# A mixing block on one core: the first phase's side transfers are issued by GpSimd instead of SP

## The chip, the core and the metric

The kernel runs on one core of a Trainium2 chip. A core has a matrix engine (TensorE, PE in the rows), a vector engine (VectorE, DVE), a scalar engine (ScalarE, ACT), GpSimd (POOL) and SyncE (SP), each with its own queue of instructions that it takes in order, and 16 DMA engines that move data between the chip's memory and the core. A transfer is issued by an instruction in the queue of one of the engines; here SP and GpSimd issue them all. The metric is the device time of one execution, in microseconds.

## The reference

One layer of a hybrid block: 2048 latent tokens and 256 context tokens of 1024 features. All arithmetic is fp32.

```
h_lat = rmsnorm(x_lat, norm1) * (1 + sc1) + sh1          # h_ctx likewise
q, k, v, gg, lr, lx, lg, su = split(h @ w_in)            # one input projection
gla  = gla_mixer(q, k, v, lr)       # gated linear attention, both directions
lru  = rglru_mixer(lx)              # short convolution, gated linear recurrence, both directions
s5   = s5_mixer(su)                 # 16 groups of 16 channels, 64 complex states each, both directions
mix  = concat(gated gla, gated lru, gated s5) @ w_out
x    = x + g1 * mix
h2   = rmsnorm(x, norm2) * (1 + sc2) + sh2
x    = x + g2 * (square(relu(h2 @ w1)) @ w2)             # MLP, 4096 wide
out  = rmsnorm(x, final_norm)
```

Each scan over the latent tokens starts from the final state of the context's scan, so it needs results of the input projection from far apart, and the backward directions need the last tokens first.

## The kernel before

**Products.** Every fp32 product of the projections is done as three products of split operands (`mm3`, L323 to L326): a weight tile is loaded by SP (`wsplit`, L318), ScalarE rounds it to its upper part (L319), VectorE takes the lower part (L320), and TensorE adds three matmuls into one accumulator. There are 2 raw buffers of weights, 2 of upper and 3 of lower parts.

**First phase** (up to about 850 us). The main stream is the input projection (`in_proj`) in four segments of 512 latent tokens and the context, followed by the output projection of the last segment (`out_proj(3)`). A finished accumulator (2 of them, `acc`) is copied by ScalarE into one of EV = 3 evacuation tiles (`evac`, L331) and stored to DRAM scratch: the parts su, lx, k, q, gg and lg by GpSimd (`put`, L343 to L355), the values v and the decay ranks by SP (`v_cols`, L385 and L394). Beside it run side streams, which read that scratch back:

- `xstream`: preparation of S5's matrices and phase tables (`s5_prep`, `s5_tables`; stores at L730 to L734 and L761), then 16 groups, one after the other (`s5_run`; loads at L770 to L774, matmuls at L783 and L820 to L824, the store of the result y at L829). A group takes 3 of 6 work slots, so two are in flight.
- `ystream`, `ystream2`: the first part of GLA by pairs of blocks (`gla_prep`, L873 to L953), with GpSimd's small copies at L906 to L913.
- the RG-LRU (`lru`, load L465, store L508), modulation vectors (`mod_rest`, weights loaded at L277), and the read-out of the last segment (`read_out(3)`, L1064 to L1142).

**Second phase**: the MLP of segments 3, 2, 1 and 0, with the RG-LRU's backward direction, read-out and output projection of the next segment beside it.

**Order.** `Streams` emits a step of a side stream whenever it is behind the main stream by planned step times. The tile framework then orders each engine's instructions by priority and by its own estimate of when operands are there, so that moving transfers to another queue also moves instructions on other engines. Each engine's queue goes strictly in order: an instruction that waits (a transfer whose source isn't written, or whose target buffer is in use) holds all that stand behind it. Transfers of one queue share 8 semaphores in turn, so each also waits for the eighth before it.

The lines that the prediction speaks of, as they stand before:

```
G.dma_start(dst[s][rows, :], e)                                       # L355 gg, lg, k, q
S.dma_start(v_d[s][sl, c * 256:(c + 1) * 256], ev[:, 0:256])          # L385 values
S.dma_start(tb, tb_d[g])                                              # L774 S5 tables of a group
S.dma_start(y_d[g // 8][:, gg * 16:(gg + 1) * 16, :, :], yo)          # L829
G.tensor_copy(c0s[:, :, two], hb_(s2)[:, :, :, 0])                    # L906
```

Of the kernel before, what the change touches and what calls it, by code (L numbers as in the profile page):

```python
# [8 lines left out]
F32 = mybir.dt.float32  # L9
# [33 lines left out]
# columns of the packed per-feature vector table  # L43
# [9 lines left out]
# W_in column tiles of 128 features  # L53
COLS = ["su0", "su1", "lx0", "lx1", "k0", "k1", "q0", "q1", "gg0", "gg1", "gg2", "gg3", "lg0", "lg1"]
WIDX = {n: i for i, n in enumerate(COLS)}
VN = 272         # half of v and the decay ranks of one direction


class Streams:
    """Emits a main and several side streams of instructions in step.  # L60

    A stream yields the time that its step takes, or the name of an event that has to be emitted first."""
# [10 lines left out]
    def step(self, limit):  # L73
        """One step of the side stream that is furthest behind; False if none is ready before `limit`."""
# [16 lines left out]
    def run(self, main):  # L91
        """`main` with the side streams."""
# [26 lines left out]
def hybrid_block(ctx: ExitStack, tc: tile.TileContext, xT, ctxT, cc, cct, wmodA, wmodT, pv, win, wva, wvb, upw, lrini, lruw, s5v, gluw,  # L119
# [27 lines left out]
    # ---------------------------------------------------------------- constants  # L147
# [53 lines left out]
    # ---------------------------------------------------------------- pools of the first phase  # L201
# [4 lines left out]
    def slots(tag, size, bufs):  # L206
        """A rotating workspace of `bufs` slots of `size` floats a partition."""
# [25 lines left out]
    # ---------------------------------------------------------------- adaLN vectors  # L233
# [3 lines left out]
    # silu(c) on every partition, for the products that run along the free axis  # L237
# [8 lines left out]
    def mod_first():  # L246
        """shift and scale of the first norm, latent and context"""
# [80 lines left out]
    # ---------------------------------------------------------------- input projection  # L328
# [40 lines left out]
    def v_cols(c, chunks):  # L369
        """Half of the values, token by token, with the decay ranks of one direction."""  # L370
        with tc.high_priority(WP):
            ws = [wsplit(ip, wv[c][:, j * 4 * VN:(j + 1) * 4 * VN], [4, VN], "w", WA) for j in range(2)]
        for s in chunks:
# [3 lines left out]
            for b in range(nb):  # L377
# [5 lines left out]
                with tc.high_priority(WP):  # L383
                    ev = evac(acc, VN)
                    S.dma_start(v_d[s][sl, c * 256:(c + 1) * 256], ev[:, 0:256])  # L385
# [1058 lines left out]
```

## Time and profile before

| | |
|---|---|
| Median of 3 runs | 2480.51 us (2476.40 to 2482.62) |
| Span of the profiled execution | 2482.1 us |
| TensorE busy | 2347.2 us (95%) |
| VectorE busy | 1610.0 us (65%) |
| ScalarE busy | 1169.2 us (47%) |
| GpSimd busy | 100.7 us (4%), 141 instructions |
| Transfers by SP's queue (hardware_dynamic) | 346.20 MB, 44.1% of the 16 engines' span |
| Transfers by GpSimd's queue (software_dynamic) | 15.93 MB, 1.9% |

The page gives the busy time of each engine and cuts the span into slices; the slices show a first third in which TensorE is not full and its clock is granted at less than full speed in pieces, and then a long stretch in which it is full. An issue of a transfer is written as DMA_DIRECT2D; on SP and in waits of SP the queue is called SPq. "L355 ... gg<-ev" reads: line 355, written tile or tensor gg, read tile ev.

### The profile page before, as it was taken

How to read it: one execution, taken by the hardware profiler on the slowest of the kernel's cores; microseconds unless marked ns; L12 is line 12 of the kernel's file. 1: busy time of each engine (PE TensorE's matmuls, PEld its weight loads, DVE VectorE, ACT ScalarE, POOL GpSimd, SP SyncE). 2: the span in 40 equal slices, each digit the busy share in tenths (PEclk: the TensorE clock that was granted, in tenths of full speed). 3: DMA queues.
4: the chain of work that ended last, by engine and by line, in shares of the span. 5: the costliest groups of instructions: out<-in, count | busy, mean ns of one | idle time of the engine just before them, and what ended most of it. 6: DMA issues, size and time to landing. Idle time of an engine off the chain costs nothing.

```text
span 2482.1 us, 29891 instructions
## 1 busy us (share of the span) xinstructions
PE 2347.2 (95%) x10992; PEld 1886.0 (76%) x10992; DVE 1610.0 (65%) x2698; ACT 1169.2 (47%) x1704; POOL 100.7 (4%) x141
## 2 busy tenths in 40 slices
PE   7779999898887899999999999999999999999997
PEld 3668777877675677888877788887778888888886
DVE  6886878726786766565576656557655655655555
ACT  3764567436555645343355534336543433433333
POOL 1020111002100000000000000000000000000000
PEclk9989999999998999999999999999999999999999
DMA  7666777557775643322355322336522232333221
GB/s 258 209 201 208 223 238 227 168 174 207 253 240 181 206 135 120 101 94 93 100 177 162 118 86 93 102 102 202 159 85 94 94 102 87 126 102 102 94 94 51
DMA packets 189107, 364.03 MB, mean 147 GB/s; under 512 B 35200, under 2 KB 104144, under 8 KB 187920
## 3 DMA queue, kind: packets, MB, share of 16 engines
q1 hardware_dynamic: 183872, 346.20, 44.1%
q0 software_dynamic: 5088, 15.93, 1.9%
q8 instruction: 86, 1.41, 0.2%
q14 instruction: 61, 0.50, 0.1%
HBM read 299.76 MB, written 62.75 MB: 146 GB/s over the span
## 4 chain that ended last, share of the span: by engine, by line
PE 64%; ACT 5%; DVE 5%; DMA 3%; issue 2%; SPq 1%; POOL 0%; DVEq 0%; ACTq 0%; POOLq 0%
PE acc L324 10%; PE acc L326 9%; PE acc L325 9%; PE sa L324 9%; PE sa L325 9%; PE sa L326 9%; PE sb L324 2%; PE sb L326 2%; PE sb L325 2%; DVE wL L320 1%; ACT wH L319 1%; PE sb L1146 1%; DMA t<-lru 1%; DMA t<-kk_d 0%; DMA wR<-in_wout_dram 0%
## 5 line engine op out<-in xcount | busy, mean ns | idle before, releaser
L319 ACT CAST wH<-wR 128x1024 fp32r<-128x1024 f32 (+1 forms) x353 | 370.9, 1051 | 903.9 <-PE sa L325 432.8
L324 PE MATMUL acc<-hH,wH 128*128 128x512 f32 (+1 forms) x1576 | 629.6, 400 | 24.8 <-ACT hH L303 9.2
L320 DVE TENSOR_TENSOR wL<-wR,wH 128x1024 fp32r<-128x1024 f32 (+1 forms) x353 | 427.3, 1222 | 346.5 <-ACT wH L319 342.0
L326 PE MATMUL acc<-hH,wL 128*128 128x512 f32 (+1 forms) x1576 | 620.1, 394 | 3.2 <-DVE wL L320 3.1
L325 PE MATMUL acc<-hL,wH 128*128 128x512 f32 (+1 forms) x1576 | 617.7, 392 | 1.2 <-DVE hL L307 0.8
L1257 DVE SCALAR_TENSOR_TENSOR xa<-sa,modl,xa 128x512 f32<-128x512 f32 (+1 forms) x520 | 383.1, 741 | 197.5 <-PE sa L326 194.8
L324 PE MATMUL sa<-sH,wH 128*128 128x512 f32 (+1 forms) x1040 | 403.9, 389 | 4.6 <-DVE xa L1257 4.2
L326 PE MATMUL sa<-sH,wL 128*128 128x512 f32 (+1 forms) x1040 | 402.2, 387 | 0.0
L325 PE MATMUL sa<-sL,wH 128*128 128x512 f32 (+1 forms) x1040 | 401.9, 386 | 0.0
L324 PEld LDWEIGHTS acc<-hH,wH 128*128 128x128 f32 x1576 | 299.8, 191 | 95.3 <-ACT hH L303 10.3
L325 PEld LDWEIGHTS acc<-hL,wH 128*128 128x128 f32 x1576 | 300.1, 191 | 70.8 <-issue 6.2
L326 PEld LDWEIGHTS acc<-hH,wL 128*128 128x128 f32 x1576 | 299.5, 190 | 70.8 <-DVE wL L320 5.2
L324 PEld LDWEIGHTS sa<-sH,wH 128*128 128x128 f32 x1040 | 195.2, 188 | 49.2 <-DVE xa L1257 9.3
L326 PEld LDWEIGHTS sa<-sH,wL 128*128 128x128 f32 x1040 | 195.3, 188 | 40.8
L325 PEld LDWEIGHTS sa<-sL,wH 128*128 128x128 f32 x1040 | 195.4, 188 | 40.6 <-DVE sL L1233 0.8
L1233 DVE TENSOR_TENSOR sL<-sr,sH 128x512 fp32r<-128x512 f32 x128 | 88.2, 690 | 27.6 <-ACT sH L1232 27.5
L325 PE MATMUL acc<-wL,hH 128*128 128x272 f32 x288 | 87.8, 305 | 8.8 <-DVE wL L320 8.7
L324 PE MATMUL acc<-wH,hH 128*128 128x272 f32 x288 | 89.2, 310 | 2.0 <-ACT ev L331 1.9
L331 ACT COPY ev<-acc 128x512 f32<-128x512 f32 (+2 forms) x96 | 47.5, 495 | 85.1 <-issue 41.0
L326 PE MATMUL acc<-wH,hL 128*128 128x272 f32 x288 | 86.5, 301 | 0.0
L1232 ACT CAST sH<-sr 128x512 fp32r<-128x512 f32 x128 | 78.8, 617 | 10.8 <-PE sa L326 9.0
L1231 ACT ACTIVATE sr<-sr 128x512 f32<-128x512 f32 x128 | 80.8, 632 | 3.4
(402 smaller groups left out, 2717.2 us busy)
## 6 DMA issues: line engine op xcount, KB each, us to landing
wR<-in_w_dram SPq DMA_DIRECT2D x256, 512.0 KB
wR<-in_win_dram SPq DMA_DIRECT2D x54, 512.0 KB
wm<-in_wmodT_dram SPq DMA_DIRECT2D x32, 512.0 KB
wR<-in_wout_dram SPq DMA_DIRECT2D x32, 512.0 KB
wm<-in_wmodA_dram SPq DMA_DIRECT2D x8, 1024.0 KB
x<-in_xT_dram SPq DMA_DIRECT2D x8, 1024.0 KB
w<-pk_d SPq DMA_DIRECT2D x16, 512.0 KB
xa<-in_xT_dram SPq DMA_DIRECT2D x32, 256.0 KB
```

The lines of the kernel that those rows point to most:

```text
L319: A.copy(Hf, raw)
L320: V.tensor_tensor(Lf, raw, f32(Hf), OP.subtract)
L324: T.matmul(acc, wH, hH, start=first, stop=False)
L325: T.matmul(acc, wH, hL, start=False, stop=False)
L326: T.matmul(acc, wL, hH, start=False, stop=last)
L331: A.copy(e, acc)
L1146: T.matmul(ps, gw[:, k, ct * P:(ct + 1) * P], sg[k], start=k == 0, stop=k == 1)
L1231: A.activation(r, r, AF.Square)
L1232: A.copy(sH, r)
L1233: V.tensor_tensor(sL, r, f32(sH), OP.subtract)
L1257: V.scalar_tensor_tensor(xa[:, m, a0:a1], acc, modl[:, 40 + m:41 + m], xa[:, m, a0:a1], OP.mult, OP.add)
```

## The change

In the first phase the transfers of the S5, GLA and RG-LRU streams, the stores of values and decay ranks, and the loads of the last segment's read-out are issued by GpSimd (`G`) instead of SP (`S`). SP keeps weights, tokens and constants, and in the second phase everything that it had. For `lru`, `back_step` and `read_out` the queue is now an argument, since both phases call them. All other edits remove comments.

```diff
-                    S.dma_start(v_d[s][sl, c * 256:(c + 1) * 256], ev[:, 0:256])
+                    G.dma_start(v_d[s][sl, c * 256:(c + 1) * 256], ev[:, 0:256])
...
-    def lru(d, order, wl=wl):
+    def lru(d, order, wl=wl, dq=G):
...
-                S.dma_start(xw[ct], src[ct * P:(ct + 1) * P, t0:t0 + n + 3])
+                dq.dma_start(xw[ct], src[ct * P:(ct + 1) * P, t0:t0 + n + 3])
...
-            S.dma_start(pk_d[gs, :, j * W:(j + 1) * W].rearrange("g p m -> p g m"),
+            G.dma_start(pk_d[gs, :, j * W:(j + 1) * W].rearrange("g p m -> p g m"),
...
-        S.dma_start(ur[:, 0:32], su_c[:, ch, :])
-        S.dma_start(ur[:, 32:288], su_l[:, ch].rearrange("s h r w -> s h (r w)"))
-        S.dma_start(pk, pk_d[g][:, 0:1024])
-        S.dma_start(tz, pk_d[g][:, 1024:])
-        S.dma_start(tb, tb_d[g])
+        G.dma_start(ur[:, 0:32], su_c[:, ch, :])
+        G.dma_start(ur[:, 32:288], su_l[:, ch].rearrange("s h r w -> s h (r w)"))
+        G.dma_start(pk, pk_d[g][:, 0:1024])
+        G.dma_start(tz, pk_d[g][:, 1024:])
+        G.dma_start(tb, tb_d[g])
...
-        S.dma_start(y_d[g // 8][:, gg * 16:(gg + 1) * 16, :, :], yo)
+        G.dma_start(y_d[g // 8][:, gg * 16:(gg + 1) * 16, :, :], yo)
...
-                S.dma_start(qq_d[(blk - 2) // 2], qd)
-                S.dma_start(kk_d[(blk - 2) // 2], kd)
+                G.dma_start(qq_d[(blk - 2) // 2], qd)
+                G.dma_start(kk_d[(blk - 2) // 2], kd)
...
+        dq = G if s == 3 else S
...
-            st.add(chain(lru(1, [s - 1], wide), read_out(s - 1), out_proj(s - 1)), RO)
+            st.add(chain(lru(1, [s - 1], wide, S), read_out(s - 1), out_proj(s - 1)), RO)
```

**SP's queue at the third S5 group, before.** The names: y is the S5 result, w_5283 and w_5282 the third group's work slots, qq_d and kk_d GLA's decayed queries and keys, wR a raw weight tile, pk_d and tb_d S5's matrices and tables.

```order
L829 DMA y_0_111<-w_5130 8x16x256
L770 DMA w_5283<-su_c_76 128x1x32
L917 DMA qq_d_115<-wg_5158 128x1024
L771 DMA w_5283<-su_l_75 128x1x256
L918 DMA kk_d_116<-wg_5155 128x1024
L318 DMA wR_6139<-in_win_dram 128x1024
L772 DMA w_5282<-pk_d_113 128x1024
L917 DMA qq_d_115<-sq_5182 128x1024
L918 DMA kk_d_116<-x_5180 128x1024
L318 DMA wR_6231<-in_win_dram 128x1024
L773 DMA w_5283<-pk_d_113 128x384
L774 DMA w_5283<-tb_d_114 128x320
```

**GpSimd's queue at the same loads, now**; c0s, x2s and a1s are the targets of GLA's small copies, gg an evacuation store of the input projection.

```order
L772 DMA w_5282<-pk_d_113 128x1024
L355 DMA gg_3_98<-ev_5679 128x512
L912 COPY a1s_158<-wg_5157 64x4x2
L913 COPY a1s_158<-wg_5157 64x4x2
L906 COPY c0s_156<-ssum_5181 128x4x2
L907 COPY x2s_157<-ssum_5181 64x4x2
L909 COPY x2s_157<-x_5180 64x4x2
L773 DMA w_5283<-pk_d_113 128x384
L774 DMA w_5283<-tb_d_114 128x320
```

The two weight loads and the four GLA stores no longer stand between the third group's loads; a store of the input projection and GLA's copies do.

**GpSimd's queue at the stores of lg of segment 1, before.** These rows are the input projection's evacuation stores, with two GLA copies.

```order
L355 DMA gg_1_96<-ev_3555 128x512
L355 DMA lg_1_100<-ev_3629 128x512
L355 DMA lg_1_100<-ev_3663 128x512
L346 DMA su_l_75<-ev_3777 128x8x64
L906 COPY c0s_156<-wg_3013 128x4x2
L907 COPY x2s_157<-wg_3013 64x4x2
L346 DMA su_l_75<-ev_3821 128x8x64
```

**The same queue from the same store on, now**; sf_d are GLA's forward states.

```order
L355 DMA gg_1_96<-ev_3555 128x512
L953 DMA sf_d_118<-fs_2980 64x512
L906 COPY c0s_156<-wg_3013 128x4x2
L907 COPY x2s_157<-wg_3013 64x4x2
L355 DMA lg_1_100<-ev_3629 128x512
L732 DMA pk_d_113<-w_3372 128x2x512
L909 COPY x2s_157<-wg_3012 64x4x2
L730 DMA pk_d_113<-w_3509 16x2x384
L912 COPY a1s_158<-wg_3013 64x4x2
L913 COPY a1s_158<-wg_3013 64x4x2
L730 DMA pk_d_113<-w_3509 16x2x384
L917 DMA qq_d_115<-wg_3014 128x1024
```

The copy L906 of the GLA block wg_3013 has moved ahead of three stores of the input projection, and the first of them now stands behind it.

**ScalarE's queue around the exponential L910 of the same GLA block, before**; acc are the main stream's accumulators in the order of the projection (3600, 3638, 3752, 3796, 3834).

```order
L331 COPY ev_3777<-acc_3752 128x512
L303 ACTIVATE hH_3670<-x_3672,modl_71 128x256 x2
L319 CAST wH_3885<-wR_3884 128x1024
L331 COPY ev_3821<-acc_3796 128x512
L920 ACTIVATE bd_3092<-x2s_157 64x8
L910 ACTIVATE wg_3013<-wg_3012,sc16_155 128x1024
```

**The same queue, now.**

```order
L331 COPY ev_3629<-acc_3600 128x512
L920 ACT_TABLE_LOAD
L920 ACTIVATE bd_3092<-x2s_157 64x8
L714 COPY w_3372<-sa_3380 128x256
L726 COPY w_3509<-sa_3499 16x2x240
L725 COPY w_3509<-sa_3500 16x2x256
L910 ACTIVATE wg_3013<-wg_3012,sc16_155 128x1024
```

The exponential stood behind the evacuation of acc_3796 and now stands behind that of acc_3600, three accumulators earlier.

## Rows read from the trace of the kernel before

**Rows 1.** The page: span and busy time of each engine.

```profile
span 2482.1 us, 29891 instructions
PE 2347.2 (95%) x10992; PEld 1886.0 (76%) x10992; DVE 1610.0 (65%) x2698; ACT 1169.2 (47%) x1704; POOL 100.7 (4%) x141
```

**Rows 2.** Busy table by stage: stretch, length, busy us per engine, clock, DMA share, GB/s.

```profile
0.00:340.00 340.00, 290.92 (x1471) 217.51 (x1472) 255.77 (x684) 186.15 (x298) 41.61 (x58) 0.94 0.69 220
340.00:560.00 220.00, 205.49 (x1086) 170.19 (x1085) 141.38 (x279) 119.53 (x191) 28.91 (x39) 0.96 0.66 198
560.00:850.00 290.00, 242.27 (x1230) 192.70 (x1228) 216.11 (x426) 173.35 (x280) 26.49 (x39) 0.94 0.71 219
850.00:2482.00 1632.00, 1608.49 (x7210) 1305.64 (x7208) 996.79 (x1313) 690.18 (x939) 3.71 (x6) 1.00 0.35 112
```

**Rows 3.** Waits of TensorE, 0 to 850 us: total us, times, longest.

```profile
PE sa L823 <- DVE w L814: 18.9, 13, 5.2
PE sb L928 <- issue: 15.1, 4, 5.3
```

**Rows 4.** Waits of SP's queue, 36 to 843 us.

```profile
SPq L318 <- DVE wL L320: 150.6, 56, 7.6
SPq L385 <- ACT ev L331: 58.5, 30, 5.4
```

**Rows 5.** Timeline of one weight load and its cast: start us, us, engine, line.

```profile
209.61 0.33 SPq L318 DMA_DIRECT2D wR<-in_win_dram  x1
...
235.27 1.05 ACT L319 CAST wH<-wR 128x1024 fp32r<-128x1024 f32 x1 [1.20 <-PE acc L326]
```

**Rows 6.** GpSimd's stores at L355 and L346: duration ns (min/median/max), then landing.

```profile
L355 POOL DMA_DIRECT2D gg<-ev x16: 540/540/548, 303.4 to 709.6; - x16
...
DMA to landing us min/median/max: 2.3/3.5/6.4
...
L346 POOL DMA_DIRECT2D su_l<-ev x8: 892/902/903, 111.4 to 567.4; - x8
```

**Rows 7.** Timeline at the third S5 group's loads, SP and VectorE.

```profile
617.45 0.63 SPq L829 DMA_DIRECT2D y<-w  x1
...
626.86 1.21 DVE L908 TENSOR_TENSOR x<-ssum 128x1024 f32<-128x1024 f32 x1
...
636.15 0.44 SPq L774 DMA_DIRECT2D w<-tb_d  x1
...
641.76 0.49 DVE L790 TENSOR_TENSOR w<-sa,w 128x320 f32<-128x320 f32 x1 [6.52 <-DMA w<-tb_d]
```

**Rows 8.** Chain that ended last, 540 to 860 us: start, us, what.

```profile
636.15 5.51 DMA w<-tb_d
...
678.53 4.44 DMA w<-tb_d
```

**Rows 9.** Timeline of a later S5 group's table load and its first use.

```profile
715.72 0.43 SPq L774 DMA_DIRECT2D w<-tb_d  x1
...
722.54 0.48 DVE L790 TENSOR_TENSOR w<-sa,w 128x320 f32<-128x320 f32 x1
```

**Rows 10.** Timeline, 353 to 403 us: VectorE, ScalarE, GpSimd and SP, chosen rows.

```profile
353.57 0.75 DVE L605 SCALAR_TENSOR_TENSOR w<-w 128x576 f32<-128x576 f32 x1
...
382.70 0.57 ACT L331 COPY ev<-acc 128x512 f32<-128x512 f32 x1
...
383.57 0.54 POOL L355 DMA_DIRECT2D lg<-ev  x1 [7.66 <-ACT ev L331]
...
386.83 0.42 SPq L734 DMA_DIRECT2D pk_d<-w  x1
...
400.27 0.58 ACT L331 COPY ev<-acc 128x512 f32<-128x512 f32 x1
...
402.00 3.38 POOL L906 COPY c0s<-wg 128x8 f32<-128x8 f32 x1 [3.18 <-DVE wg L904]
```

**Rows 11.** Waits of GpSimd's queue, 36 to 843 us.

```profile
POOL c0s L906 <- DVE wg L904: 59.8, 7, 14.3
```

More of the change, by code (lines that the diff above doesn't have):

```diff
@@ L393, in v_cols @@
             dst, t0 = (lrt_c, 0) if s == "c" else (lrt_l, s * SEG)
-            S.dma_start(dst[32 * c:32 * c + 16, t0 + c:t0 + c + nb * P], le)
+            G.dma_start(dst[32 * c:32 * c + 16, t0 + c:t0 + c + nb * P], le)
             done.add(f"v{c}_{s}")
@@ L507, in lru @@
                 if s != "c":
-                    S.dma_start((hf_d, lr_d)[d][s][rows, :], h)
+                    dq.dma_start((hf_d, lr_d)[d][s][rows, :], h)
             done.add(f"lru{d}_{s}")
@@ L760, in s5_tables @@
         for j in range(2):
-            S.dma_start(tb_d[gs, :, j * NCOL:(j + 1) * NCOL].rearrange("g p m -> p g m"), tab[:, j])
+            G.dma_start(tb_d[gs, :, j * NCOL:(j + 1) * NCOL].rearrange("g p m -> p g m"), tab[:, j])
     def s5_run(g):
@@ L882, in gla_prep @@
             ksrc = k_d[s][:, bl].rearrange("(h d) t -> d h t", d=64)
-            S.dma_start(flat(kd[0:64]), ksrc)
-            S.dma_start(flat(kd[64:128]), ksrc)
+            G.dma_start(flat(kd[0:64]), ksrc)
+            G.dma_start(flat(kd[64:128]), ksrc)
             if s != "c":
@@ L887, in gla_prep @@
                 qsrc = q_d[s][:, bl].rearrange("(h d) t -> d h t", d=64)
-                S.dma_start(flat(qd[0:64]), qsrc)
-                S.dma_start(flat(qd[64:128]), qsrc)
+                G.dma_start(flat(qd[0:64]), qsrc)
+                G.dma_start(flat(qd[64:128]), qsrc)
             for j in range(2):
@@ L922, in gla_prep @@
             yield 4
-            S.dma_start(s1.rearrange("p (b e) -> p b e", b=2), v_d[s][bl, :].rearrange("(b p) e -> p b e", p=P))
+            G.dma_start(s1.rearrange("p (b e) -> p b e", b=2), v_d[s][bl, :].rearrange("(b p) e -> p b e", p=P))
             halves = [slice(i * 512, (i + 1) * 512) for i in range(2)]
@@ L938, in gla_prep @@
             yield 3
-            S.dma_start(ds_d[two].rearrange("b p e -> p b e"), s2[64:128].rearrange("p (b e) -> p b e", b=2))
+            G.dma_start(ds_d[two].rearrange("b p e -> p b e"), s2[64:128].rearrange("p (b e) -> p b e", b=2))
             if blk:
@@ L952, in gla_prep @@
                     fst["s"] = new
-                    S.dma_start(sf_d[blk + i - 1], new)
+                    G.dma_start(sf_d[blk + i - 1], new)
             done.add(f"fs_{blk + 1}")
@@ L959, in gla_ends @@
         le = wg(2, rows=48)
-        S.dma_start(le[:, 0:1], lrt_c[:, CTX:CTX + 1])
-        S.dma_start(le[:, 1:2], lrt_l[:, SEQ:SEQ + 1])
+        G.dma_start(le[:, 0:1], lrt_c[:, CTX:CTX + 1])
+        G.dma_start(le[:, 1:2], lrt_l[:, SEQ:SEQ + 1])
         tm, tn = wg(8), wg(8)
@@ L1018, in hybrid_block, with back_step @@
     bst = {}
-    def back_step(ss, blk):
+    def back_step(ss, blk, dq):
         rows = slice(64, 128)
         def step(dst, src, at):
-            S.dma_start(dst[rows], ds_d[at])
+            dq.dma_start(dst[rows], ds_d[at])
             for h in range(HEADS):
@@ L1030, in back_step @@
             first = side.tile([P, SEG], F32, name="first", tag="first")
-            S.dma_start(first[rows], ds_d[1])
+            dq.dma_start(first[rows], ds_d[1])
             step(ss, first, 0)
@@ L1063, in read_out @@
                 tl[b] = qs, ks, vs, gs_ = ws(s, 4)
-                S.dma_start(h4(gs_), gg_d[s][:, bl].rearrange("(h p) t -> p h t", p=P))
+                dq.dma_start(h4(gs_), gg_d[s][:, bl].rearrange("(h p) t -> p h t", p=P))
                 for t, d in ((qs, qq_d), (ks, kk_d)):
-                    S.dma_start(h4(t), d[blk // 2].rearrange("p (h b t) -> p h b t", h=4, b=2)[:, :, b % 2, :])
-                S.dma_start(vs, v_d[s][bl, :])
+                    dq.dma_start(h4(t), d[blk // 2].rearrange("p (h b t) -> p h b t", h=4, b=2)[:, :, b % 2, :])
+                dq.dma_start(vs, v_d[s][bl, :])
                 A.activation(gs_, gs_, AF.Silu)
@@ L1072, in read_out @@
                 ss = sst[b] = ws(s, 1, "ss")[0]
-                S.dma_start(ss[0:64], sf_d[blk])
-                back_step(ss, blk)
+                dq.dma_start(ss[0:64], sf_d[blk])
+                back_step(ss, blk, dq)
                 sf, sb = sb_tile(), sb_tile()
@@ L1118, in read_out @@
             g_, h_, f_ = ws(s, 3)
-            S.dma_start(f_, hf_d[s][rows, :])
-            S.dma_start(g_, lg_d[s][rows, :])
-            S.dma_start(h_, lr_d[s][rows, :])
+            dq.dma_start(f_, hf_d[s][rows, :])
+            dq.dma_start(g_, lg_d[s][rows, :])
+            dq.dma_start(h_, lr_d[s][rows, :])
             A.activation(g_, g_, AF.Gelu_apprx_tanh)
@@ L1133, in read_out @@
             y_, u_ = ws(s, 2)
-            S.dma_start(y_.rearrange("p (t w) -> p t w", w=64), y_d[ct][:, :, s, :].rearrange("t c w -> c t w"))
-            S.dma_start(u_.rearrange("p (t w) -> p t w", w=64), su_l[:, rows, s, :].rearrange("t c w -> c t w"))
+            dq.dma_start(y_.rearrange("p (t w) -> p t w", w=64), y_d[ct][:, :, s, :].rearrange("t c w -> c t w"))
+            dq.dma_start(u_.rearrange("p (t w) -> p t w", w=64), su_l[:, rows, s, :].rearrange("t c w -> c t w"))
             V.scalar_tensor_tensor(y_, u_, col("s5d", ct), y_, OP.mult, OP.add)
@@ L1141, in read_out @@
         gw = gw.rearrange("p (k m) -> p k m", k=2)
-        S.dma_start(gw, gluw.rearrange("p (k m) -> p k m", k=2))
+        dq.dma_start(gw, gluw.rearrange("p (k m) -> p k m", k=2))
         for ct in range(2):
```

6 lines of the change are left out of this document (3 added, 3 removed).

## The prediction, made before the changed kernel ran

> **What bounds the kernel now.** I read the page first, then the busy table by stage, then the waits of TensorE and of SP's queue, and last the instructions around single transfers. The page has TensorE busy in 2347.2 of 2482.1 us [rows 1], so at most 135 us are to be had by any change to waits. The table by stage says where: from 850 us on TensorE works 1608.49 of 1632 us at clock 1.00, and before 850 it works 290.92, 205.49 and 242.27 us, 738.7 of 850 [rows 2]. The shortfall there is 111.3 us, and the granted clock of those stages is 0.94 to 0.96. The second phase keeps its queue (only the first phase's transfers move), so whatever happens must happen in those 850 us; what is gained or lost there shifts the rest as a block.
>
> What does TensorE wait for in the 850 us? Not for transfers of weights: the two longest sums are S5's read-out products (L823), which wait 18.9 us in 13 pieces for VectorE's L814, and GLA's transposes (L928), 15.1 us with no releaser that the trace names [rows 3]. A transfer can only stand behind one of these.
>
> SP's queue does look blocked: from 36 us on it waits 150.6 us, in 56 pieces, at weight loads whose raw buffer VectorE still reads (L318), and 58.5 us at value stores (L385) [rows 4]. Everything behind such a load waits too. For the weights themselves this costs nothing: a load issued at 209.61 is cast at 235.27 [rows 5], some 25 us later, and a wait for VectorE to free the buffer is no wait for SP. So a lighter SP buys the weights about nothing. What it can buy is that side transfers no longer stand behind weight loads.
>
> **The change part by part.**
>
> *Issue cost.* By the two orders 393 issues leave SP for GpSimd. On GpSimd a plain store takes 540 ns, lowest, median and longest 540, 540, 548; the store in 64-element pieces 892 to 903 ns [rows 6]. 393 x 0.54 = 212 us, at 0.9 us 354 us; beside the 100.7 us that GpSimd is busy now [rows 1] this is 37 to 53% of the first 850 us. SP needs about the same for such an issue: 0.63 us for the y store at 617.45 [rows 7]. So the queue can carry it, and the issues themselves cost nothing as long as order, not throughput, decides.
>
> *Landing.* The trace shows landing on the software queue for its own stores: 2.3 to 6.4 us, median 3.5 [rows 6]. S5's loads on SP's queue take 5.51 and 4.44 us on the chain that ended last [rows 8]. So a load lands between 3.2 us sooner (5.51 against 2.3) and 2.0 later (4.44 against 6.4), by the median 1 to 2 us sooner. In the steady part of the S5 stage the table load of a group goes out at 715.72 and VectorE uses it at 722.54 [rows 9]: 6.8 us, so 1 to 2 us either way is hidden there. I take 0, bounds -3 and +4 over the whole stage.
>
> *S5 loads no longer behind weights: the gain.* Ahead of the third group's loads the y store goes out at 617.45, the table load only at 636.15, since two weight loads and four GLA stores stand between on SP (the order above). VectorE then stands still 6.52 us until 641.76 [rows 7], and this transfer is on the final chain [rows 8]. In the new order the table load stands on GpSimd behind small GLA copies, the last of which follows VectorE's L908, which ends at 626.86 + 1.21 = 628.1 [rows 7]; issued at 628.6 and landing 5.5 us later it is there at 634.1, before VectorE starts to wait (641.76 - 6.52 = 635.2). So up to 6.5 us go. As the groups after it are 9 to 10 us apart and bound by L823's chain of vector work, a shift of one group is passed on to the last, but another wait may come late next: GLA's L928 at the same time. I take -5, bounds -7 and 0.
>
> *S5 preparation earlier.* Its second store of a matrix is ready when L605 ends, 353.57 + 0.75 = 354.3, and goes out at 386.83, 32 us late [rows 10], which holds a work slot. In the new order the GLA and S5 preparation moves forward, by three input-projection tiles in the ScalarE order above. The preparation ends long before the first group needs it (which waits for the last su tile), so this gains on TensorE's side waits only: the 340 to 560 stage lacks 220 - 205.49 = 14.5 us in all [rows 2]. Earlier side work may sit in front of main products as well as fill gaps; I take 0, bounds -6 and +4.
>
> *Stores of the main stream behind waiting side transfers: the loss.* GpSimd already issues the stores of gg, lg, su, lx, k and q; v joins them. They stood among few instructions; now they stand behind S5 and GLA transfers that wait for VectorE, and a queue goes in order. The worst place by the times of before: lg's store that went out at 383.57 now stands behind the copy L906, which before ended at 402.00 + 3.38 = 405.4 [rows 10], so 22 us late. There are three evacuation buffers and two accumulators. The first of four evacuations in a row comes at 382.70, the fourth at 400.27 [rows 10]; the fourth needs the first one's buffer, free at about 405.6 + 3.5 = 409.1, 9 us late, of which the spare accumulator takes a tile's 6 us ((400.27 - 382.70)/3): 3 us of stall. But L906's input is itself three tiles earlier in the new order: on ScalarE the exponential that follows it stood behind the evacuation of acc_3796, now behind that of acc_3600, 400.27 - 382.70 = 17.6 us, and the 22 us shrink to about 4. Between 340 and 500 us I count three stretches of that sort in the new order. Bounds 0 and +27 (three times the 9 us, if side work gets no earlier and no accumulator is spare); I take +2, near the end where the side work does move.
>
> *The end of the phase* (read-out and output projection of the last segment): token loads now wait on GpSimd's transfers, hidden behind the S5 gate. I take 0, bound +4.
>
> **Sum.** 0 - 5 + 0 + 2 + 0 = -3 against the profiled execution's span of 2482.1 us, which lies 1.6 us above the median of 2480.51; so about 2477 by the median. A difference under 0.3%, 7.4 us, is about what a measurement of this kernel can't tell from none.
>
> On that queue the rows show issues that stay at 540 ns with VectorE busy 65% of the span [rows 1, 6], landings of at most 6.4 us, and small copies of GpSimd that do stretch, to 3.38 us for one of 128x8 elements [rows 10]. A page of the Trainium skill speaks against the change: SBUF — State Buffer, section "Who interferes with whom", says that a transfer issued by GpSimd can be starved of its descriptors while VectorE runs certain operations that take both ports, and that one issued from elsewhere is immune. By that rule the sum would be that of rival 4 below; by the issue rows it stays at -3.
>
> **Rivals.**
> 1. *Hidden anyway (0, about 2480):* the 6.5 us of the third group come back as a wait for L814 or L928. For: L823's waits for VectorE are the largest sum [rows 3]. Against: the table load is on the final chain.
> 2. *Faster, 2462:* side streams that are no longer held fill TensorE's gaps; the 560 to 850 stage lacks 290 - 242.27 = 47.7 us [rows 2]. A third of that, 16 us, and 2 us of the clock's lower stretches: -18. For: SP stood still 209 us on its two main waits. Against: most of the gaps name VectorE.
> 3. *Slower, 2502: main-stream stores stuck on GpSimd.* One mechanism, at 340 to 500 us, priced above at +27 at its upper end; I give +22, since the first tile of each stretch has its spare accumulator. It decides from the point where a store is later than three evacuations, about 18 us. For: the queue goes in order, and L906 alone already waited 59.8 us in 7 pieces [rows 11]. Against: side work moves forward.
> 4. *Slower, 2497: the software queue lags.* If every S5 group loses 1 us beyond its slack, 16 groups give +16; it needs landings over 6.8 us [rows 9], and the trace has 6.4 at most [rows 6]. The flat issue time speaks against it. The page named above would have it this way.
>
> **Chances.** Forecast (2470 to 2486) 0.32; rival 1 0.18; rival 2 0.25; rival 3 0.17; rival 4 0.08. Faster by over 0.3%: rival 2 nearly whole, 0.24, and the forecast's lower end 0.10, together 0.34. Slower: rivals 3 and 4, 0.23, and 0.03 from the upper ends, 0.26. The rest, 0.40, is within. The range leaves out the outer fifth: 2461 (rival 2, a little over its price) to 2500 (most of rival 3).
>
> **What would show it.** Right: the third group's table load issued before 632 and no wait of VectorE for it; S5's last y store 3 to 7 us earlier; weight loads at the same distance to their cast; the time from the last y store to the second phase unchanged. Wrong: TensorE or ScalarE waiting for evacuation buffers at 340 to 500 us (rival 3); loads of S5 on GpSimd landing 7 us or more after issue (rival 4); shortfall of TensorE between 560 and 850 down by over 10 us (rival 2).

## The result: slower by 43 us, and the profile after

The changed kernel takes 2521.51 us (median of 4 runs, 2518.98 to 2525.12), the kernel before 2478.45 (4 runs, 2476.18 to 2482.62): ratio 1.0177 [1.0163, 1.0191]. The forecast of 2477 and its range up to 2500 are both missed, on the slow side.

The page of the changed kernel, its span, its busy times and its two DMA queues (packets, MB, share of 16 engines):

```profile
span 2520.5 us, 29912 instructions
PE 2359.0 (94%) x10992; PEld 1892.0 (75%) x10992; DVE 1611.4 (64%) x2698; ACT 1168.0 (46%) x1705; POOL 322.0 (13%) x534
...
q1 hardware_dynamic: 117568, 267.43, 32.2%
q0 software_dynamic: 32096, 94.72, 11.8%
```

Against [rows 1] the span is 38.4 us longer: TensorE is busy 11.8 us more (2359.0 against 2347.2 for the same 10992 matmuls), and idle 26.6 us more (161.5 against 134.9). The busy table by stage (start and end, length, busy us and count of PE, PEld, DVE, ACT, POOL, granted clock, DMA share, GB/s):

```profile
0.00:340.00 340.00, 278.84 (x1388) 211.69 (x1389) 249.99 (x682) 169.41 (x274) 98.56 (x163) 0.91 0.67 223
340.00:560.00 220.00, 197.52 (x1048) 159.73 (x1046) 142.06 (x277) 124.29 (x197) 90.15 (x146) 0.96 0.56 176
560.00:890.00 330.00, 275.72 (x1360) 215.04 (x1359) 224.80 (x432) 187.10 (x299) 129.62 (x219) 0.95 0.65 206
890.00:2520.00 1630.00, 1606.89 (x7202) 1305.55 (x7200) 994.58 (x1309) 687.22 (x936) 3.71 (x6) 1.00 0.34 112
```

The second phase is what it was in [rows 2] (23.1 us without matmul here, 23.5 there). The first 340 us hold 83 matmuls fewer than before, at a mean granted clock of 0.91 instead of 0.94, that is, more of them at the lower of its two levels (1.2 and 2.4 GHz). So the loss lies in the first phase, and it begins in its first third, long before S5's scan.

Two lines of the waits of VectorE between 36 and 890 us in the changed kernel (us in total, times, longest), then the same line of the kernel before between 36 and 843 us, which was not read for the prediction:

```profile
DVE wL L320 <- ACT wH L319: 80.0, 28, 9.7
DVE wm L278 <- DMA wm<-in_wmodT_dram: 39.1, 16, 8.9
```
```profile
DVE wm L278 <- DMA wm<-in_wmodT_dram: 26.2, 11, 4.4
```

L278 is the modulation product on VectorE, one of 32 steps, each of which needs a load into a single buffer (MB = 1). None of these instructions or loads changed its queue. One of the waits in the timeline of the changed kernel (start, duration, engine, instruction, in brackets the idle time before it), VectorE's rows and then TensorE's:

```profile
303.73 1.23 DVE L278 SCALAR_TENSOR_TENSOR wm<-wm,cbl 128x1024 f32<-128x1024 f32 x1 [2.17 <-DMA wm<-in_wmodT_dram]
...
309.91 1.23 DVE L278 SCALAR_TENSOR_TENSOR wm<-wm,cbl 128x1024 f32<-128x1024 f32 x1 [4.76 <-DMA wm<-in_wmodT_dram]
...
311.29 1.22 DVE L320 TENSOR_TENSOR wL<-wR,wH 128x1024 fp32r<-128x1024 f32 x1
```
```profile
312.57 0.80 PE L326 MATMUL acc<-hH,wL 128*128 128x512 f32 x1 [5.33 <-DVE wL L320]
313.16 0.63 PE L324 MATMUL acc<-hH,wH 128*128 128x512 f32 x1
...
318.49 0.40 PE L325 MATMUL acc<-hL,wH 128*128 128x512 f32 x1
```

Two modulation steps stand close together, VectorE holds still 4.76 us for the second one's load, the split of a weight tile (L320) stands behind it, and TensorE waits 5.33 us for that. The wait is paid for twice: after it the products take 0.63 us each at the lower clock, and only from 318 us on 0.40 us again.

### The profile page after: what moved, and what is told of

It is laid out like the page before. It is cut to its first block, busy times and chain, and to the rows that moved or that the text cites. A ratio compares the mean times of both kernels' runs of the same rounds, so it can differ in the third digit from the quotient of the medians.

```text
span 2520.5 us, 29912 instructions
## 1 busy us (share of the span) xinstructions
PE 2359.0 (94%) x10992; PEld 1892.0 (75%) x10992; DVE 1611.4 (64%) x2698; ACT 1168.0 (46%) x1705; POOL 322.0 (13%) x534
## 3 DMA queue, kind: packets, MB, share of 16 engines
q0 software_dynamic: 32096, 94.72, 11.8%
## 4 chain that ended last, share of the span: by engine, by line
PE 61%; ACT 4%; DVE 2%; issue 2%; DMA 2%; POOL 1%; SPq 0%; DVEq 0%; ACTq 0%; POOLq 0%
PE sa L324 9%; PE acc L324 9%; PE sa L325 9%; PE acc L326 9%; PE sa L326 9%; PE acc L325 9%; PE sb L324 2%; PE sb L326 2%; PE sb L325 2%; PE sb L1147 1%; DMA t<-lru 1%; PE mm L1092 0%; DMA t<-kk_d 0%; PE mm L1093 0%; ACT wH L319 0%
## 5 line engine op out<-in xcount | busy, mean ns | idle before, releaser
L320 DVE TENSOR_TENSOR wL<-wR,wH 128x1024 fp32r<-128x1024 f32 (+1 forms) x353 | 427.2, 1223 | 349.2 <-ACT wH L319 346.5
L326 PE MATMUL acc<-hH,wL 128*128 128x512 f32 (+1 forms) x1576 | 623.1, 396 | 9.0 <-DVE wL L320 9.0
L326 PE MATMUL sa<-sH,wL 128*128 128x512 f32 (+1 forms) x1040 | 402.8, 387 | 0.0
L326 PEld LDWEIGHTS acc<-hH,wL 128*128 128x128 f32 x1576 | 300.4, 191 | 78.8 <-DVE wL L320 12.1
L326 PEld LDWEIGHTS sa<-sH,wL 128*128 128x128 f32 x1040 | 195.8, 188 | 40.9
L326 PE MATMUL acc<-wH,hL 128*128 128x272 f32 x288 | 87.2, 303 | 0.0
```

The source lines that it names most:

```text
L320: V.tensor_tensor(Lf, raw, f32(Hf), OP.subtract)
L326: T.matmul(acc, wL, hH, start=False, stop=last)
```

## The experiments

The change does two things at once: another queue carries 393 transfers, and the scheduler, which sees that, puts the instructions of every engine in another order. Theory Q: the queue costs the time. Theory O: the order costs it. Theory L of the expectations is Q by way of loads that land later. By the programs' count 192 of the transfers are S5's, 95 GLA's and 106 the rest (values, ranks, RG-LRU, read-out); the expectations below name other numbers, which were miscounted.

### Parts of the change, each with the order that the scheduler makes of it

Edits, each alone: the transfers of S5; those of GLA; the rest; all stores while the loads stay on SP.

```
-  S.dma_start(<transfers of the part>)
+  G.dma_start(<transfers of the part>)
```

> Only S5's transfers (L730 to L774, L829) are issued by GpSimd; GLA, RG-LRU, values and read-out stay on SP as before. Theory L, loads of the software queue land later than those of SP and TensorE waits for them: S5's loads gave TensorE 5.1 us of waits at L783 for pk_d and ScalarE 13.5 us at L777, so 8 to 15 us slower than before. Theory O, the price is the order (what the planner hoists when SP is light, and GpSimd's queue in which side transfers stand before copies and stores): S5 alone takes a third of the moved issues and leaves GLA's order alone, so 0 to 5 us slower. If the streams add up, this, gla_only and rest_only together give 43 us.

> Only GLA's transfers (L873 to L961) are issued by GpSimd. Theory L: TensorE's waits at L936 for the loads of v were 14.4 us with all moved, with some microseconds of low clock behind them: 12 to 20 us slower than before. Theory O: GLA's transfers stand in GpSimd's queue before its own small copies, on which ScalarE waits (L920); 15 to 25 us slower with waits at L920 and in the weights' split (L319, L320), not at L936.

> Only the values' and decay ranks' stores, the RG-LRU and the last segment's read-out are issued by GpSimd; S5 and GLA stay on SP. Theory L: few loads of the main path, 0 to 6 us slower. Theory O: the stores of values leave SP, where they waited 58.5 us ahead of weight and modulation loads; the modulation loads come closer together and VectorE waits for them, 5 to 15 us slower.

> All stores of the change on GpSimd, all loads of the side streams (S5 L770 to L774, GLA L873 to L889, L923, L960, L961, RG-LRU L465, read-out) back on SP. Theory L: the loss is in the loads, so at most 8 us slower than before, and no waits of TensorE at L936 for v. Theory O: the queue of GpSimd is nearly as crowded with transfers that wait for VectorE, and SP is lighter as well: 20 to 40 us slower.

Measured: S5 alone 2510.23 us against 2482.35, 1.0113 [1.0095, 1.0131]; GLA alone 1.0114 [1.0096, 1.0132]; the rest alone 1.0120 [1.0103, 1.0138]; the stores alone 1.0112 [1.0093, 1.0131]. Four disjoint or overlapping parts cost 28 to 30 us each, and three that make up the whole come to 85 us where the whole costs 43. That is no price per transfer or per group, and it is neither loads nor stores. It points to something that each edit brings: another order. Of the eight ranges expected, only theory O's for the stores (20 to 40) holds what was measured. The kept trace of GLA alone has signs of both theories: VectorE waits 40.9 us in 19 pieces for modulation loads (26.2 in 11 before), and TensorE 16.5 us in 7 at L936 for GLA's loads of v, as theory L said, where before it waits for none.

### Queue and order apart, by holding the order

To set the order by hand, each of the following kernels carries a table of it, and consecutive instructions of an engine are tied so that they are issued in that order (it adds lines: L299, L341, L347, L376 and L850 are L278, L320, L326, L355 and L829 of the kernel before, 21 lines down).

```
+  for i in sorted(instructions, key=place_in_table):
+      if i.engine in last:
+          tc.add_manual_dep(i, last[i.engine], <issue order only, no semaphore>)
+      last[i.engine] = i.name
```

`new_queue_old_order`: the changed kernel, held to the order of the kernel before. `old_queue_new_order`: the kernel before (all on SP), held to the order of the changed one. `before_rx31`: the kernel before with a slightly different pace of one side stream and the order that results, as a test whether any reshuffle costs such a sum.

```
-  RX, RY, ... = 3.0, 0.8, ...
+  RX, RY, ... = 3.1, 0.8, ...
```

> The changed kernel's queues (393 transfers on GpSimd) with the order of the kernel before held on every engine: PE, ACT and DVE row by row as before, and GpSimd's and SP's queues as the sub-orders of the order before. Theory O (the new order that the scheduler makes of the change costs the time): within 8 us of the kernel before, or faster, since SP is lighter and nothing else moved. Theory L (the software queue's later landing and GpSimd's issue cost): 25 to 45 us slower than before, with waits of TensorE at L936 for v and at L783 for pk_d.

> All 393 transfers back on SP, but every engine in the changed kernel's order (PE, ACT and DVE row by row as in it; SP's queue takes the transfers of both queues in the changed kernel's planned sequence). Theory O: 25 to 45 us slower than before. Theory L: within 8 us of before or a little slower, no waits at L936 for v.

> The kernel before, all queues as before, with one planning constant moved by 3% (RX, the pace of the S5 stream beside the main stream, 3.0 to 3.1): only the order changes. Theory O in its general form (the order before is a narrow optimum of the constants, so that any reshuffle costs): 10 to 30 us slower. If only the order that this change makes is bad: within 8 us.

Measured: the new queue in the old order 2521.72 us against 2479.52, 1.0161 [1.0135, 1.0187]; the old queue in the new order 2520.68, 1.0153 [1.0130, 1.0176]; the reshuffle 0.9994 [0.9980, 1.0008]. Both theories are right, the queue by itself for 42 us, the order by itself for 41, and they do not add: both together cost 43. On the new order the queue makes no difference that these runs can tell (1.0177 against 1.0153, the intervals overlap); on the old order it costs all.

Where the time goes differs. The y stores of the 16 S5 groups mark the S5 stage (durations of the issue, first and last start): before, after, old queue in new order, new queue in old order.

```profile
L829 SPq DMA_DIRECT2D y<-w x16: 592/615/638, 586.3 to 779.4; - x16
```
```profile
L829 POOL DMA_DIRECT2D y<-w x16: 613/645/664, 614.4 to 813.7; - x16
```
```profile
L850 SPq DMA_DIRECT2D y<-w x16: 599/618/641, 615.5 to 815.1; - x16
```
```profile
L850 POOL DMA_DIRECT2D y<-w x16: 636/646/657, 598.6 to 815.4; - x16
```

From first to last store the four take 193.1, 199.3, 199.6 and 216.8 us; the first store comes 28.1, 29.2 and 12.3 us later than before. The new order loses most of its time ahead of the S5 stage, on whichever queue; the new queue in the old order loses more than half of it (23.7 us) inside the stage.

### What of the order: the modulation stream

Theory M: the modulation steps come too early and too close together (they start between 79.4 and 502.5 us before, between 77.5 and 338.5 after). Edits: the order of before with only its 32 modulation steps (L277 to L279) at their places in the changed kernel; the same with S5's steps; and the kernel before with the pace of the modulation stream changed by its constant.

```
-  place_in_table[i] = place_before(i)
+  place_in_table[i] = place_after(i) if i is a modulation step (an S5 step) else place_before(i)
```
```
-  RX, RY, RZ, RM, ... = 3.0, 0.8, 4.0, 8.0, ...
+  RX, RY, RZ, RM, ... = 3.0, 0.8, 4.0, 12.0, ...
```

> All queues and the order as before, but the 32 steps of the modulation stream (load L277, VectorE's L278 and L279) at the places beside the main products that the changed kernel's order gives them: the last at 338 us instead of 502, with one buffer. Theory M (the order's price is VectorE waiting in order for these loads, 48.0 us in 19 waits in old_queue_new_order against 26.2 in 11 before): 10 to 25 us slower than before. If the price of the order lies in S5's and GLA's earlier steps instead: 0 to 5 us slower.

> All queues and the order as before, but S5's steps (preparation, tables, runs) at the places beside the main products that the changed kernel's order gives them. The modulations' places alone gave 20 us, the whole new order 40. If the other half is S5's: 10 to 22 us slower; if it is GLA's or comes with the mixture: 0 to 6 us.

> The kernel before with the pace of the modulation stream RM at 12 instead of 8: the steps come later (the last by 1939 main products of the first phase instead of 1780), all queues as before. Theory M (close modulation loads cost since VectorE waits for them in order): 2 to 8 us faster than before. If the price of old_order_new_mod came from elsewhere: within 3 us.

Measured: new places of the modulation steps 2499.89 us, 1.0086 [1.0066, 1.0106], +20; S5's steps 2615.73, 1.0541 [1.0517, 1.0564]; the pace constant 2487.52, 1.0027 [1.0017, 1.0038], +6.5. The first makes the waits of the changed kernel with no transfer on another queue. VectorE's wait line, one of its stalls, and TensorE behind it, all of this kernel:

```profile
DVE wm L299 <- DMA wm<-in_wmodT_dram: 40.6, 16, 5.8
```
```profile
319.23 1.23 DVE L299 SCALAR_TENSOR_TENSOR wm<-wm,cbl 128x1024 f32<-128x1024 f32 x1 [4.59 <-DMA wm<-in_wmodT_dram]
...
324.67 1.23 DVE L299 SCALAR_TENSOR_TENSOR wm<-wm,cbl 128x1024 f32<-128x1024 f32 x1 [4.01 <-DMA wm<-in_wmodT_dram]
...
326.05 1.23 DVE L341 TENSOR_TENSOR wL<-wR,wH 128x1024 fp32r<-128x1024 f32 x1
```
```profile
327.33 0.79 PE L347 MATMUL acc<-hH,wL 128*128 128x512 f32 x1 [7.69 <-DVE wL L341]
```

40.6 us in 16 waits, as the changed kernel's 39.1 in 16, against 26.2 in 11. In the profiled execution TensorE is idle 14.3 us more than before (149.2 against 134.9), about as much as VectorE's waits have grown (14.4), and busy 8.8 us more for the same matmuls (2356.0 against 2347.2), at a mean granted clock of 0.83 instead of 0.93 between 100 and 200 us. So about half of the order's 41 us is this stream, if the parts of the order add up, which was not tested. The other half is not settled: the mixture with S5's steps loses 135 us, more than either order that it is mixed from, so it tells only that two orders can't be pasted together there. The constant went the wrong way: it costs 6.5 us where a gain or nothing was expected. Its trace fits theory M all the same, for the stream ends later (542.7 us) and VectorE still waits 8.5 us longer for its loads than before:

```profile
DVE wm L278 <- DMA wm<-in_wmodT_dram: 34.7, 14, 6.0
```

So the place of a step among the others matters, not the mean distance.

### What of the queue: which transfers, and what they stand behind

With the order of before held, S5's, GLA's and the remaining transfers were moved one group at a time.

```
-  S.dma_start(<transfers of the group>)
+  G.dma_start(<transfers of the group>)    # and in_order(tc) with the table of before
```

> The order before held on every engine, only S5's transfers on GpSimd. Theory B (a moved transfer stands in GpSimd's queue behind copies and stores of other streams that wait: in new_queue_old_order an S5 y store was ready at 625.3 and issued at 644.6, behind GLA's copy L906 that waited 12.8 us): 15 to 30 us slower than before, nearly all of it after 560 us. Rival I (GpSimd's issue cost and the software queue itself, in proportion to the transfers moved): S5 has 184 of 393 transfers, so about 19 us, spread over the phase.

> The order before held, only GLA's transfers on GpSimd. Theory B: GLA's transfers stand behind GLA's own copies, where they would wait anyway, and the stores of the input projection behind them; 0 to 10 us slower. Rival I: 72 of 393 transfers, about 8 us. Both lie together here; what tells is held_s5_queue and held_rest_queue against it.

> The order before held, only the stores of values and decay ranks, the RG-LRU and the last segment's read-out on GpSimd. Theory B: stores of values depend on the main stream alone and pass few waiting copies; the read-out's loads stand behind few: 0 to 8 us slower. Rival I: 137 of 393 transfers, about 14 us.

Measured, against 2480.20 us: S5 2504.44, 1.0097 [1.0079, 1.0116], +24; GLA 2488.36, 1.0038 [1.0024, 1.0051], +8; the rest 2485.21, 1.0021 [1.0012, 1.0030], +5. In one order the parts do add: 37 of the 42. They don't go by the count (24, 8 and 5 us for 192, 95 and 106 transfers), as rival I would have it, and S5's lie in the stage: its y stores run from 590.1 to 800.6 us, 3.8 late at the first and 21.2 at the last. What arrives late there, in the kernel with all 393 moved (L811 is the first use of the tables, L790 before, and L804 that of the matrices, L783 before):

```profile
DVE w L811 <- DMA w<-tb_d: 17.5, 3, 8.1
```
```profile
PE sa L804 <- DMA w<-pk_d: 11.9, 6, 5.0
```

In the kernel before VectorE waits 6.5 us in one piece for a table, and TensorE at L783 for no matrix.

What holds S5's transfers on GpSimd? Theory B: GLA's small copies (L906 to L913), which wait for VectorE there. Theory E: the stores of the input projection's evacuated tiles (L343 to L355), which wait for main products. Edits, in the order of before: copies on VectorE, with and without S5's move.

```
-  G.tensor_copy(c0s[:, :, two], hb_(s2)[:, :, :, 0])      # and the others of L906 to L913
+  V.tensor_copy(c0s[:, :, two], hb_(s2)[:, :, :, 0])
```

> As held_s5_queue (the order before held, only S5's 192 transfers on GpSimd; 24 us slower), but GLA's small copies L906 to L913 are on VectorE at the same places of the held order, so that they don't stand in GpSimd's queue. Theory B: S5's transfers no longer stand behind copies that wait; the loss falls to 5 to 14 us, less what before_copies_dve shows for the copies. Rival I (issue cost and the software queue itself): the loss stays at 20 to 28 us.

> The base for held_s5_copies_dve: all queues and the order as before, GLA's small copies L906 to L913 on VectorE instead of GpSimd. Both theories: within 5 us of before.

Measured: 2498.95 us, 1.0067 [1.0052, 1.0082], with its own base at 2477.84, 0.9985 [0.9975, 0.9996]: S5's move still costs 21 us where it cost 24. Theory B falls, and the loss is where rival I had it (20 to 28). The timeline of GpSimd in this kernel shows what stands in front of them (L376 stores an evacuated tile, L850 is S5's y store, L791 to L795 are the next group's loads), and below it ScalarE's row that makes the y:

```profile
621.70 0.55 POOL L376 DMA_DIRECT2D gg<-ev  x1 [15.92 <-ACT ev L352]
622.24 0.64 POOL L850 DMA_DIRECT2D y<-w  x1
622.87 0.62 POOL L791 DMA_DIRECT2D w<-su_c  x1
...
629.13 0.59 POOL L376 DMA_DIRECT2D gg<-ev  x1 [5.04 <-ACT ev L352]
629.71 0.57 POOL L793 DMA_DIRECT2D w<-pk_d  x1
640.02 0.54 POOL L376 DMA_DIRECT2D lg<-ev  x1 [9.73 <-ACT ev L352]
640.55 0.55 POOL L794 DMA_DIRECT2D w<-pk_d  x1
641.09 0.55 POOL L795 DMA_DIRECT2D w<-tb_d  x1
```
```profile
617.33 0.28 ACT L848 COPY w<-sa 128x128 f32<-128x128 f32 x1
```

The y is there at 617.61 and goes out at 622.24, behind a store of gg for whose tile GpSimd waits 15.92 us. The loads of the next group go out in three bits, each behind the next evacuated tile; L794 and L795 stand behind a store of lg for which GpSimd is idle 9.73 us. On SP, in the kernel before, the same loads stood behind weight loads, of which none waited longer than 7.3 us between 560 and 785 us.

If E (B2 in the expectations) holds, the evacuation stores on SP give the 21 us back. Edits, with the copies on VectorE and the order of before: these stores on SP, alone; with S5's transfers on GpSimd; and with all side streams' transfers there. The last one moves 347 of the 393: the 46 stores of values and decay ranks belong to the main stream and stay on SP.

```
-  G.dma_start(dst[s][rows, :], e)       # L343, L346, L352, L355
+  S.dma_start(dst[s][rows, :], e)       # in the last kernel L385 and L394 (values, ranks) as well
```

> The base for it: the order before held, GLA's copies on VectorE, the evacuation stores on SP with everything else, GpSimd with next to no transfers. If SP's queue can take waiting stores without loss (it takes those of v): within 5 us of before. If theory B2's blocking is symmetric, S5's transfers now stand behind the same waiting stores on SP: 10 to 25 us slower, and held_s5_alone is the faster of the two.

> The order before held; GLA's copies on VectorE as in held_s5_copies_dve; now the evacuation stores (su, lx, k, q, gg, lg; L343 to L355) are on SP as well, so that S5's 192 transfers have GpSimd's queue nearly alone. Theory B2 (S5's transfers stand behind evacuation stores that wait for the main products: a gg store waited 15.9 us at 621.70 with the y store right behind it, and lg 9.7 us at 640.02 with the table load behind it): the loss against before_evsp falls from 21 to 0 to 7 us. Rival I (the software queue itself): it stays at 15 to 25 us.

> As held_s5_alone, but all side streams (S5, GLA, RG-LRU, read-out) on GpSimd, and all stores of the main stream (evacuations, values, decay ranks) on SP: the change with the main stream's stores kept apart, in the order before. Theory B2 for all streams: the 41 us of new_queue_old_order fall to 0 to 12. If side streams block each other, it stays at 15 to 30.

Measured, against 2484.58 for the kernel before: the stores on SP alone 2484.77 us, 1.0004 [0.9996, 1.0013]; S5 with them 2496.01, 1.0046 [1.0032, 1.0060], +11 instead of 21; all side streams 2497.54, 1.0058 [1.0044, 1.0072], +13 instead of 42. The 11 lie between the two ranges expected, the 13 just above theory B2's. The kernel before in its own order, held and otherwise unchanged, was not run; with the copies on VectorE it lies at 0.9985, with the stores on SP too at 1.0004, so holding an order costs little. The y stores of the last one, and those of the stores on SP alone:

```profile
L850 POOL DMA_DIRECT2D y<-w x16: 633/647/661, 593.4 to 790.9; - x16
```
```profile
L850 SPq DMA_DIRECT2D y<-w x16: 598/624/647, 586.4 to 779.3; - x16
```

The stage takes 197.5 us instead of 216.8, where its base takes 192.9. So 29 of the queue's 42 us go when the main stream's stores and the copies no longer share the side transfers' queue. At most 3 of them are the small copies (24 against 21), and some may be the 46 stores that went back to SP (values, ranks, RG-LRU and read-out together cost 5).

That the waiting stores are the cause does not follow. The kernel with the stores on SP alone has the same transfers behind the same stores, in SP's queue. The y store of the same group stands behind the same store there:

```profile
616.61 0.33 SPq L376 DMA_DIRECT2D gg<-ev  x1
...
617.79 0.64 SPq L850 DMA_DIRECT2D y<-w  x1
```

That y is there at 612.79 and goes out 5.0 us later, as on GpSimd (4.6), and VectorE waits 7.4 us for the next group's table load (8.1 on GpSimd). Yet that kernel loses nothing, where a blocking that works alike on both queues was expected to cost 10 to 25 us. So on SP these stores cost the side transfers nothing, and what GpSimd's queue adds to them no run tells.

Some 11 to 13 us stay with a queue that has none of these stores in front; over half of them come ahead of the S5 stage (first y store 7.0 us late). Three causes are open. Issues take longer on GpSimd (below): with S5 alone there the last 14 groups take 169.7 us where the base takes 161.5, 0.6 us a group, and the five loads of a group take 0.6 us longer to issue (3.1 against 2.5 us, medians added); that the two agree is no proof. Side transfers wait behind one another: GpSimd waits 169.8 us in 8 pieces at S5's own store L753, which is L732 of the kernel before. And single landings are late, up to 9.6 us for a table. Of all kernels tried only the copies on VectorE without any move come out ahead of the kernel before, by 0.0015 of its time [0.0004, 0.0025].

## Why the prediction was wrong, step by step

**What bounds the kernel** held: all is decided in the first phase, and the second is unchanged.

**Issue cost 0** held as to the queue's room: 393 issues do not fill it, it is idle most of the first phase. That SP needs the same for an issue held for the y store alone (645 ns on GpSimd, 615 on SP), which the prediction had picked; its own rows of the table load on SP say 0.44 us [rows 7], and GpSimd takes longer (before, then after):

```profile
L774 SPq DMA_DIRECT2D w<-tb_d x16: 430/430/504, 519.8 to 763.5; - x16
```
```profile
L774 POOL DMA_DIRECT2D w<-tb_d x16: 541/576/613, 538.4 to 789.9; - x16
```

By the medians the five loads of an S5 group (L770 to L774) take 3.0 us to issue instead of 2.5, an estimate of 8 us over 16 groups if all of it lay on the chain. It doesn't show in the changed kernel, whose stage is as long as that of the old queue in the same order (199.3 and 199.6 us).

**Landing 0** held for S5 by the medians. The page has S5's matrices land 5.1 us after issue, on GpSimd's queue (KB each, median us):

```profile
w<-pk_d POOLq DMA_DIRECT2D x16, 512.0 KB, 5.1
```

The longest landing of S5's loads (L770 to L774) is 7.0 us, just at the prediction's mark for rival 4, the lagging software queue; the table load, whose slack was 6.8, lands in at most 6.8. The rule of the Trainium skill named with it (SBUF — State Buffer, "Who interferes with whom") is not seen at work: issues of S5's loads and y stores take 541 to 664 ns (lowest of L774, longest of L829) beside a VectorE that is busy 68% of the stage from 560 to 890 us. The rule speaks of certain operations of VectorE, which these rows don't tell apart, so this is no test of it. What remains of 11 to 13 us could still hold such a cost; no run excludes it.

GLA's loads had no term in the sum. In the changed kernel TensorE waits at L936 for its loads of v, 14.4 us in 7 pieces, of which this is the largest line:

```profile
PE sb L936 <- DMA wg<-v: 10.5, 5, 3.8
```

Before it waits there for no load, and with the old queue in the new order 5.6 us in 4. Since that kernel is as slow within the noise, these waits don't add to its time one for one.

**S5 loads no longer behind weights, -5**: the gain came at the third group, but from the order and not from the queue, and it was lost again. In the third group the y store leaves GpSimd at 644.59, the table load at 653.22, 8.6 us later instead of 18.7, and VectorE, which waited 6.52 us for it in [rows 7], no longer does (GpSimd's rows, then VectorE's, of the changed kernel):

```profile
644.59 0.63 POOL L829 DMA_DIRECT2D y<-w  x1 [4.81 <-ACT w L827]
...
653.22 0.55 POOL L774 DMA_DIRECT2D w<-tb_d  x1
```
```profile
658.38 0.49 DVE L790 TENSOR_TENSOR w<-sa,w 128x320 f32<-128x320 f32 x1 [0.55 <-PE sa L783]
```

The third group's own y store comes 20.7 us after the second group's (665.30 after 644.59) instead of 32.9 (650.37 after 617.45). But with all transfers on SP, in the new order, the table load leaves no later (L850 and L795 are L829 and L774 there):

```profile
644.70 0.63 SPq L850 DMA_DIRECT2D y<-w  x1
...
650.15 0.43 SPq L795 DMA_DIRECT2D w<-tb_d  x1
```

There the third group takes 21.2 us. With the new queue in the old order the table load leaves 14.6 us after the y store (659.26 after 644.64), and the group takes 32.5 us. So the gain goes with the order, on either queue. Nor is it passed on to the last group, as the prediction had it: the second group's y store stands some 27 us late already in the changed kernel, the fourth group then takes 24.6 us instead of 14.8 and the last two 26.7 instead of 18.2: the 16 groups take 199.3 us, 6.2 longer than before.

**S5 preparation earlier, 0 with bounds -6 and +4**, is the step that failed first. It priced the moves of two side streams by the idle time that they could fill, and took the rest of the order as given. The order alone, without the queue, costs 41 us, and the new places of a stream that the change doesn't touch cost 20 by themselves: VectorE's line L278, of which the prediction read no row. That line's loads land 4.5 us after issue by the page of the changed kernel, so a step that follows the last one at once waits about that long, 4.76 us in the stall above, and holds the weights' split behind it:

```profile
wm<-in_wmodT_dram SPq DMA_DIRECT2D x32, 512.0 KB, 4.5
```

The prediction did not read the two orders for a step that now meets a load that hasn't landed. Where the other half of the 41 comes from stays open, and whether a second buffer would take that wait away was not tried.

**Stores of the main stream behind waiting side transfers, +2 with bounds 0 and +27**, has the right queue and the wrong direction. The stores were not late: the trace of the changed kernel names no wait of ScalarE for an evacuation tile's store (3.3 us before), that of the new queue in the old order 8.1 us in two pieces (340 to 560 us). It is the side transfers that get later, in the S5 stage, and with these stores out of their queue 29 of the 42 us are gone. Standing behind them is not the whole of it, for on SP the same stores stand before the same transfers at no loss. In the kernel before GpSimd already waited for evacuated tiles longer than for the L906 of [rows 11], with no side transfer behind (its waits from 36 to 850 us):

```profile
POOL k L355 <- ACT ev L331: 94.8, 7, 55.7
POOL lg L355 <- ACT ev L331: 69.7, 6, 30.3
POOL gg L355 <- ACT ev L331: 65.2, 9, 13.6
```

In the changed kernel's order the queue adds 1 us by the two medians and 6 by the two ratios, which the intervals don't tell from none; why it costs so little there was not tested.

**The end of the phase, 0 with bound +4**: from the last y store to the second phase 66.8 us (813.7 to 880.47) instead of 63.3 (779.4 to 842.72), within the bound.

## What to carry to other kernels

Moving transfers to another queue under a scheduler changes the order on every engine: price the new order as a change of its own, and measure the two apart by holding the order. A queue that goes in order is idle but not free while its head waits for another stream: here a stream with a tight chain lost 10 us less (11 instead of 21) on a queue without stores that wait for another stream's products. But the same stores before the same transfers cost nothing on SP, so such a wait has a price only by trial. A step that waits in order for a single-buffered load costs as soon as two of them stand closer than the load takes, here 4.5 us.

## What the hardware showed that was not expected

The 393 transfers are fewer packets on the software queue. Of the hardware queue's 183872 packets and 346.20 MB before, 66304 packets and 78.77 MB went; the software queue got 27008 packets for 78.79 MB. The two shares together fell from 46.0% of the DMA engines' span to 44.0%, and the kernel was slower all the same.

GpSimd's small copies of GLA take 0.19 us in one place and 1.24 us in another for the same 64x8 elements. The long one lies beside an operation of VectorE (642.35 to 643.58) and ends 0.04 us after it (new queue in old order, GpSimd):

```profile
636.50 0.19 POOL L930 COPY x2s<-wg 64x8 f32<-64x8 f32 x1
...
642.38 1.24 POOL L933 COPY a1s<-wg 64x8 f32<-64x8 f32 x1 [4.04 <-ACT wg L931]
```
